# Rotary positions in an attention stage: the halves exchanged by four transfers on SyncE, with weights' high parts on ScalarE from unit three

## The chip, the core and the metric

The kernel runs on one core of a Trainium2 chip. The metric is the time of one execution on the device in microseconds (us); before the change it is 1156.18 us, the median of three runs (1155.56 to 1158.52). The core has five engines with a queue of instructions each: TensorE (PE, with its weight loads as PEld), VectorE (DVE), ScalarE (ACT), GpSimd (POOL) and SyncE (SP). Each works through its own queue in order and waits at an instruction until what this needs is there. Transfers are issued by SP or ACT and carried out by 16 DMA engines.

## The reference, cut to what matters

One inference step of a two-layer decoder with 1024 features: 512 prompt tokens and 8 sample tokens. Layer 0 mixes tokens by sliding-window attention (16 query heads of 64 values, 2 key heads, window 128, a learned sink per head), layer 1 by gated linear attention; each is followed by a gated feed-forward network with a short convolution, and each of the four sublayers by a layer norm. The change touches the attention alone, at the rotary positions, which turn each head's first and second 32 values against each other:

```python
def rope(x, pos):
    ...
    x1, x2 = jnp.split(xf, 2, axis=-1)
    rot = jnp.concatenate([-x2, x1], -1)
    return (xf * cos + rot * sin).astype(x.dtype)
```

So the rotation needs each value's partner, 32 places away in the head.

## The kernel before, in words

Tokens are split into group a (256) and group b (256 + 8). Activations lie with features on the 128 partitions and tokens along the row. Every product of weights is made at higher precision than one pass gives: a weight tile `raw` is split into a high part `wh` and a low part `wl` (`load_unit`, L146 to L162), the activations likewise, and three products of parts are summed in PSUM (`product`, L164 on).

The weights are cut into units of 128 output columns. Unit 0 makes the keys, unit 1 the values, units 2 to 9 eight query chunks of two heads each, units 10 on the output projection, and then come the feed-forward and the second layer. A unit's load is issued by SP into one of two `raw` buffers (RAWS = 2); its parts go to one of six slots (WSLOTS = 6). The high part is made by POOL for units below HIACT = 10 and by ACT from there on; DVE makes the low part. A load has to wait until DVE has finished with the unit two before, and a slot until PE has finished with the unit six before.

In the attention stage (L310 to L532) `attn_k`, `attn_v` and `attn_q` run for each unit and group. Keys and queries go through `rope` (L357 to L369), 18 times in all (keys and eight query chunks, two groups):

- ACT copies the product out of PSUM into `ra` with scale and bias (L362).
- DVE shuffles rows inside blocks of 32 partitions into `rb`, 16 places on (L364). So that partners lie 16 apart within a block of 32, the head's values are laid out in a permuted order, PERM, applied to weights, keys, cache and tables on the host.
- POOL multiplies `ra` by the cosines in place (L365), DVE multiplies `rb` by the sines (L366), POOL adds the two into `rr` (L368).

For a query chunk, ACT makes the high part of `rr` and DVE the low part in `hl` (L413, L414). Four transfers, issued by ACT, put both parts of each head below each other in `qs` (L416 to L419), 64 in all. Then PE makes scores against keys (L446, L447), DVE masks and finds the maximum (L456 to L461), ACT takes exponentials (L463), POOL and DVE normalise (L466, L469), PE transposes (L475), ACT copies (L477), POOL selects the two window halves (L481), and PE multiplies by the values (L494). The tiles `ra`, `rb`, `rr`, `hl` and `qs` have two buffers each, the accumulators `accp` four.

The program's text does not fix the order on each engine. A planner goes through the traced instructions with its own costs and writes every engine's queue in the order in which they came up in its plan; on the chip these orders are fixed. Only the loads at the start keep a given order on SP (`attn_open`, L323 to L346), the loads for units 4 and 5 as the last of them, and a few others are marked to keep program order.

Of the kernel before, what the change touches and what calls it, by code (L numbers as in the profile page):

```python
# [11 lines left out]
F32 = mybir.dt.float32  # L12
# [14 lines left out]
HD = 64  # L27
# [14 lines left out]

WSLOTS = 6
RAWS = 2
HIACT = 10

EXTRA = 1
XEND = 8
# [43 lines left out]
class Net:  # L92
# [53 lines left out]
    def load_unit(self, u, pieces=1, extra=False):  # L146
# [8 lines left out]
        for c in (slice(i * n, (i + 1) * n) for i in range(pieces)):  # L155
            nc.sync.dma_start(out=r[:, c], in_=src[:, c])
            if u >= HIACT:
                nc.scalar.activation(h[:, c], r[:, c], AF.Copy)  # L158
# [198 lines left out]
    def rope(self, g, ps, scale, bias):  # L357
        nc, n = self.nc, g.n
        tab = self.rope_t[:, :, g.c0:g.c0 + n]
        t = lambda name: self.ap.tile([P, NT - 256], F32, name=name, bufs=2)[:, :n]  # L360
        a = t("ra")
        nc.scalar.activation(a, ps, AF.Identity, scale=scale, bias=bias)  # L362
        b = t("rb")
        nc.vector.stream_shuffle(b, a, [(i + 16) % 32 for i in range(32)])  # L364
        nc.gpsimd.tensor_tensor(a, a, tab[:, 0], op=ALU.mult)  # L365
        nc.vector.tensor_tensor(b, b, tab[:, 1], op=ALU.mult)  # L366
        r = t("rr")
        nc.gpsimd.tensor_tensor(r, a, b, op=ALU.add)  # L368
        return r  # L369
# [36 lines left out]
    def attn_q(self, g, u, c):  # L406
        nc = self.nc
# [4 lines left out]
        hl = self.ap.tile([P, 2, 256], F32R, name="hl", bufs=2)  # L412
        nc.scalar.activation(hl[:, 0], r[:, :256], AF.Copy)  # L413
        nc.vector.tensor_tensor(hl[:, 1], r[:, :256], hl[:, 0].bitcast(F32), op=ALU.subtract)  # L414
        qs = self.ap.tile([P, 2, 256], F32R, name="qs", bufs=2)
        for part in range(2):  # L416
            for v in range(2):
                nc.scalar.dma_start(out=qs[64 * part:64 * part + 64, v].bitcast(F32),
                                    in_=hl[64 * v:64 * v + 64, part].bitcast(F32))  # L419
        if g.i:  # L420
            for v in range(2):
                own = slice(64 * v, 64 * v + 64)
# [2 lines left out]
        if g.i and c < 2:  # L425
            if c == 0:
                d = nc.sync.dma_start(out=self.kc[:, :, 0:127], in_=self.I["cache_k"])
            else:
                d = nc.sync.dma_start(out=self.vc, in_=self.I["cache_v"])
# [564 lines left out]

def _perm():
    d = []
    for q in range(2):
        d += list(range(16 * q, 16 * q + 16)) + list(range(32 + 16 * q, 48 + 16 * q))  # L1000
    return np.array(d)


PERM = _perm()
QROWS = np.concatenate([np.concatenate([np.arange(64) + 64 * c, np.arange(64) + 64 * (8 + c)]) for c in range(8)])


def _units(w):

    k, m = w.shape  # L1010
    return np.ascontiguousarray(w.reshape(k // P, P, m // P, P).transpose(2, 1, 0, 3).reshape(m // P, P, k))
# [6 lines left out]
def _consts():  # L1018
# [3 lines left out]
    cos, sin = np.cos(ang), np.sin(ang)  # L1022
    cos = np.concatenate([cos, cos])[PERM]
    sin = np.concatenate([-sin, sin])[PERM]
    cs = np.stack([np.tile(cos, (2, 1)), np.tile(sin, (2, 1))], 1).astype(np.float32)
# [7 lines left out]
def _layout(inp):  # L1033
# [4 lines left out]
    w, b = f["attn_w_qkv"][0], f["attn_b_qkv"][0]  # L1038
    kperm = D + np.concatenate([PERM, 64 + PERM])
    vperm = D + 128 + np.arange(128)  # L1040
    qperm = np.concatenate([np.concatenate([64 * c + PERM, 64 * (8 + c) + PERM]) for c in range(8)])
    order = np.concatenate([kperm, vperm, qperm])
    a["w_qkv"] = _units(w[:, order])
    a["cache_k"] = f["cache_k"][0][:, 1:][..., PERM].transpose(2, 3, 0, 1).reshape(P, NS, 127)

# [58 lines left out]
```

## Time and profile before

| | us |
|---|---|
| median of three runs | 1156.18 |
| the profiled execution | 1155.92 |
| its span, first to last instruction | 1154.2 |
| PE busy in the span | 1106.0 |
| DVE busy | 799.5 |
| ACT busy | 557.3 |
| POOL busy | 348.9 |

The profile shows one execution. "Busy" counts the time in which an engine works; issuing transfers and waiting at them is not counted. A view by stretches gives each engine's busy time between two points of the span. A line such as "L368 POOL ... rr<-ra,rb x18: 721/746/899" is one source line on one engine, what it writes and reads, how often, and the shortest, median and longest duration in ns. "idle before" is the time for which the engine stood idle ahead of those instructions, with what ended it. SPq and ACTq are the queues of SP and ACT, where issues of transfers appear. The chain of waits follows the work that ended last back from one releaser to the one before. The granted clock of TensorE was 0.987 of full over the span.

### The profile page before, as it was taken

The page shows a single profiled execution, that of the slowest core. Times are in us where ns is not written, and L with a number is a line of the kernel's source. Part 1 is how long each engine was busy: PE and PEld are TensorE (multiplying, and loading weights), DVE is VectorE, ACT ScalarE, POOL GpSimd, SP SyncE. Part 2 cuts the span into 40 slices and gives each one's busy share as a digit, 9 for nine tenths or more (in the row PEclk, how much of TensorE's full clock was granted, in tenths as well). Part 3 has the DMA queues.
Part 4 walks back from the last instruction along what each step waited for, and adds up shares of the span by engine and source line. Part 5 has one row for each costly group of instructions (what it writes and reads, how often), then busy time and mean ns, then how long its engine had stood idle before and what let it go on. Part 6 is the DMA issues. An engine that isn't in the chain of part 4 may idle for free.

```text
span 1154.2 us, 22951 instructions
## 1 busy us (share of the span) xinstructions
PE 1106.0 (96%) x8806; PEld 1056.4 (92%) x8806; DVE 799.5 (69%) x1663; ACT 557.3 (48%) x1212; POOL 348.9 (30%) x597
## 2 busy tenths in 40 slices
PE   8988898999999999999899999999999999999995
PEld 7987798999999999998899899889999999999994
DVE  7987769755665456568867777799756665566656
ACT  3455546533554245445545556456533553245433
POOL 4787668200011001156400100378100110010344
PEclk9999999999999999999899999999999999999998
DMA  6634122223323233243034354442323323233212
GB/s 220 177 109 133 25 80 93 92 77 126 110 92 105 97 96 106 73 133 117 29 101 129 126 187 150 142 132 69 110 89 115 108 93 109 93 102 101 74 63 75
DMA packets 53789, 122.82 MB, mean 106 GB/s; under 512 B 6792, under 2 KB 27312, under 8 KB 53680
## 3 DMA queue, kind: packets, MB, share of 16 engines
q1 hardware_dynamic: 46544, 115.41, 30.6%
q10 hardware_dynamic: 7136, 5.95, 2.1%
q8 instruction: 69, 1.13, 0.4%
q14 instruction: 40, 0.33, 0.1%
HBM read 108.67 MB, written 8.47 MB: 101 GB/s over the span
## 4 chain that ended last, share of the span: by engine, by line
PE 72%; DVE 12%; POOL 6%; DMA 4%; issue 3%; ACT 2%; ACTq 0%; SPq 0%; DVEq 0%; POOLq 0%
PE accp L191 15%; PE accp L174 15%; PE accp L173 14%; PE accp L175 14%; PE accp L192 8%; DMA vb<-dv 3%; DVE wl L161 2%; POOL x_b L298 1%; POOL x_a L298 1%; DVE u L296 1%; DVE sgla L845 1%; POOL pr L469 1%; DVE msq L276 1%; PE pv L494 1%; PE sc L767 1%
## 5 line engine op out<-in xcount | busy, mean ns | idle before, releaser
L161 DVE TENSOR_TENSOR wl<-raw,wh 128x1024 fp32r<-128x1024 f32 (+2 forms) x189 | 231.3, 1225 | 106.5 <-ACT wh L158 104.6
L158 ACT ACTIVATE wh<-raw 128x1024 fp32r<-128x1024 f32 (+1 forms) x176 | 182.9, 1039 | 212.4 <-PE accp L174 198.9
L173 PE MATMUL accp<-xh_b,wh 128*128 128x264 f32 x976 | 271.5, 279 | 2.6 <-DVE hprod L600 2.6
L174 PE MATMUL accp<-xl_b,wh 128*128 128x264 f32 x976 | 271.2, 278 | 0.2
L175 PE MATMUL accp<-xh_b,wl 128*128 128x264 f32 x976 | 270.9, 278 | 0.0
L191 PE MATMUL accp<-xs_a,wh 128*128 128x512 f32 x576 | 196.3, 382 | 0.0
L174 PEld LDWEIGHTS accp<-xl_b,wh 128*128 128x128 f32 x976 | 185.2, 190 | 3.3 <-DVE xl_b L301 0.6
L173 PEld LDWEIGHTS accp<-xh_b,wh 128*128 128x128 f32 x976 | 185.1, 190 | 3.3 <-DVE hprod L600 2.9
L175 PEld LDWEIGHTS accp<-xh_b,wl 128*128 128x128 f32 x976 | 184.8, 189 | 0.8 <-issue 0.6
L192 PE MATMUL accp<-xs_a,wl 128*128 128x256 f32 x576 | 145.4, 273 | 0.0
L173 PE MATMUL accp<-hh_b,wh 128*128 128x264 f32 x480 | 133.5, 278 | 2.6 <-ACT hh_b L198 2.6
L174 PE MATMUL accp<-hl_b,wh 128*128 128x264 f32 x480 | 134.0, 279 | 0.0
L175 PE MATMUL accp<-hh_b,wl 128*128 128x264 f32 x480 | 133.2, 277 | 0.0
L191 PEld LDWEIGHTS accp<-xs_a,wh 128*128 128x128 f32 x576 | 109.1, 189 | 11.4
L173 PE MATMUL accp<-xs_a,wh 128*128 128x256 f32 x400 | 113.1, 288 | 4.9 <-DVE x_b L217 1.1
L174 PE MATMUL accp<-xs_a,wh 128*128 128x256 f32 x400 | 112.8, 284 | 3.5 <-DVE xs_a L301 2.9
L175 PE MATMUL accp<-xs_a,wl 128*128 128x256 f32 x400 | 111.7, 282 | 2.9 <-DVE wl L161 2.9
L192 PEld LDWEIGHTS accp<-xs_a,wl 128*128 128x128 f32 x576 | 110.2, 191 | 1.9
L202 POOL COPY hist<-aext 128x2 f32<-128x2 f32 x44 | 8.9, 201 | 284.6 <-DVE aext L578 281.5
L173 PEld LDWEIGHTS accp<-hh_b,wh 128*128 128x128 f32 x480 | 91.2, 190 | 3.1 <-ACT hh_b L198 2.9
L174 PEld LDWEIGHTS accp<-hl_b,wh 128*128 128x128 f32 x480 | 91.1, 190 | 1.5 <-issue 0.3
L175 PEld LDWEIGHTS accp<-hh_b,wl 128*128 128x128 f32 x480 | 91.0, 190 | 0.2
(320 smaller groups left out, 2512.9 us busy)
## 6 DMA issues: line engine op xcount, KB each, us to landing
raw<-in_w_up SPq DMA_DIRECT2D x88, 512.0 KB, 3.4
raw<-in_w_down SPq DMA_DIRECT2D x32, 512.0 KB, 3.4
raw<-in_w_gla SPq DMA_DIRECT2D x24, 512.0 KB, 3.4
raw<-in_w_mix_o SPq DMA_DIRECT2D x16, 512.0 KB, 3.6
raw<-in_w_down SPq DMA_DIRECT2D x16, 384.0 KB, 3.0
qs<-hl ACTq DMA_DIRECT2D x64, 64.0 KB, 2.0
sgla<-in_state_gla SPq DMA_DIRECT2D x16, 256.0 KB, 2.9
vb<-dv SPq DMA_DIRECT2D x16, 256.0 KB, 3.8
```

Of the source, the lines that this page charges most:

```text
L158: nc.scalar.activation(h[:, c], r[:, c], AF.Copy)
L161: nc.vector.tensor_tensor(l[:, c], r[:, c], h[:, c].bitcast(F32), op=ALU.subtract)
L173: nc.tensor.matmul(o, h[:, ks], xh, start=k == 0, stop=False)
L174: nc.tensor.matmul(o, h[:, ks], xl, start=False, stop=False)
L175: nc.tensor.matmul(o, l[:, ks], xh, start=False, stop=k == nt - 1)
L191: both = lambda: nc.tensor.matmul(o, h[:, ks], in_turn(rs[:, k].rearrange("p t q j -> p t (q j)")), start=k == 0, stop=last)
L192: low = lambda: nc.tensor.matmul(o[:, :P], l[:, ks], in_turn(rh[:, k]), start=False, stop=False)
L276: nc.vector.scalar_tensor_tensor(q, q, 0.5, nv, op0=ALU.mult, op1=ALU.mult)
L296: nc.vector.tensor_tensor(u, x[:, m], r, op=ALU.mult)
L298: ts = nc.gpsimd.tensor_scalar(x[:, m], u, sc(m), bi(m), op0=ALU.mult, op1=ALU.add)
L469: nc.gpsimd.tensor_scalar(pr[:, b, 0:P], pr[:, b, 0:P], den[:, b:b + 1], 1.0, op0=ALU.mult, op1=ALU.mult)
L494: mm = nc.tensor.matmul(pv[64 * v:64 * v + 64, b * P:(b + 1) * P], self.vtok[:, kb, 64 * v:64 * v + 64], parts[v][w][:, b], start=i == 0, ...
```

## The change

The shuffle goes. Four transfers of 32 partitions each, issued by SP, write into `rb` the rows of `ra` with neighbouring blocks of 32 exchanged, and the head's values lie in their plain order again (PERM is the identity; the host applies it as before). The 64 transfers into `qs` are issued by SP instead of ACT. HIACT is 2 instead of 10, so that ACT rather than POOL makes the high parts of units 2 to 9, that is from the third unit on; POOL keeps those of units 0 and 1.

```diff
-HIACT = 10
+HIACT = 2
...
         a = t("ra")
         nc.scalar.activation(a, ps, AF.Identity, scale=scale, bias=bias)
         b = t("rb")
-        nc.vector.stream_shuffle(b, a, [(i + 16) % 32 for i in range(32)])
+
+        for i in range(4):
+            nc.sync.dma_start(out=b[32 * i:32 * i + 32], in_=a[32 * (i ^ 1):32 * (i ^ 1) + 32])
         nc.gpsimd.tensor_tensor(a, a, tab[:, 0], op=ALU.mult)
...
         for part in range(2):
             for v in range(2):
-                nc.scalar.dma_start(out=qs[64 * part:64 * part + 64, v].bitcast(F32),
-                                    in_=hl[64 * v:64 * v + 64, part].bitcast(F32))
+                nc.sync.dma_start(out=qs[64 * part:64 * part + 64, v].bitcast(F32),
+                                  in_=hl[64 * v:64 * v + 64, part].bitcast(F32))
...
-def _perm():
-    d = []
-    for q in range(2):
-        d += list(range(16 * q, 16 * q + 16)) + list(range(32 + 16 * q, 48 + 16 * q))
-    return np.array(d)
-
-
-PERM = _perm()
+PERM = np.arange(HD)
```

## Prediction

> **What bounds the kernel now.** I read the page first, then busy time by stretches, then the waits and the chain of waits in the attention stretch, then the tiles that the change touches, and last the timeline around the first and the last rotation.
>
> ```profile
> span 1154.2 us, 22951 instructions
> ...
> PE 1106.0 (96%) x8806; PEld 1056.4 (92%) x8806; DVE 799.5 (69%) x1663; ACT 557.3 (48%) x1212; POOL 348.9 (30%) x597
> ```
>
> TensorE is busy for 96% of the span; the other engines have room only as an average. The rotation (`rope`) lies wholly in the first stage, so the stretches come next. Their columns are start and end, length, busy time of PE, weight load, DVE, ACT and POOL, the granted clock, the DMA engines' share, and GB/s.
>
> ```profile
> core 0: us, PE busy (x) PEld busy (x) DVE busy (x) ACT busy (x) POOL busy (x), PEclk, DMA share, GB/s
> 8.00:28.00 20.00, 16.63 (x117) 14.92 (x117) 18.29 (x37) 8.31 (x21) 10.52 (x14) 0.91 0.66 213
> 28.00:124.00 96.00, 86.93 (x777) 80.37 (x777) 80.97 (x233) 51.64 (x190) 75.38 (x131) 0.98 0.47 134
> 124.00:150.00 26.00, 22.46 (x202) 20.24 (x202) 15.81 (x46) 10.96 (x43) 15.76 (x33) 0.93 0.04 11
> 150.00:1154.00 1004.00, 974.17 (x7692) 935.92 (x7690) 682.23 (x1344) 483.60 (x954) 244.72 (x413) 0.99 0.32 103
> ```
>
> From 28 to 124 us, where the attention heads are worked, PE is idle for 96 - 86.93 = 9.1 us; in the three stretches up to 150 us it is idle for 3.4 + 9.1 + 3.5 = 16.0 us. This is the ceiling on any gain, since the change takes no work from PE and touches nothing after 150 us. In the same 96 us DVE is busy for 81 and POOL for 75: three engines stand at 80 to 90% and feed one another in short steps. What ends the idle time there (total us, times, longest):
>
> ```profile
> ACT hl L413 <- POOL rr L368: 9.3, 4, 3.9
> ...
> PE pv L494 <- POOL pu L481: 6.1, 5, 2.5
> ...
> ACT ra L362 <- POOL rr L368: 4.5, 3, 2.5
> ...
> ACT hl L413 <- DMA qs<-hl: 4.1, 2, 3.4
> ```
>
> No single engine is the bound; ACT waits for POOL's sum and for its own transfers, PE for POOL's selects. The chain of waits from 28 to 120 us, and the one from 20 to 80 us, by share of the stretch:
>
> ```profile
> by line: POOL pr L469 10.2%; issue 7.5%; POOL rr L368 5.7%; POOL pl L481 5.4%; ACTq L418 5.2%; POOL pu L481 5.1%; DVE rb L366 4.8%; DVE wl L161 4.5%; DMA qs<-hl 4.5%; DVE sc L456 3.8%; ACT pr L463 3.5%; DMA raw<-in_w_qkv 3.3%; PE accp L174
> ```
>
> ```profile
> by line: POOL pr L469 9.2%; DVE wl L161 8.2%; issue 6.2%; DVE rb L366 5.8%; DVE xl_b L199 5.1%; DMA raw<-in_w_qkv 5.0%; PE accp L174 4.7%; DVE sc L456 4.6%; DVE rb L364 4.4%; PE accp L175 4.1%; PE accp L173 4.1%; POOL rr L368 3.8%; DVE hl L
> ```
>
> "ACTq L418" is ACT standing at the issue of the qs transfers: 5.2% of 92 us, 4.8 us. "DVE rb L364" is the shuffle: 4.4% of 60 us, 2.6 us.
>
> **The change, part by part.** *The shuffle leaves DVE.*
>
> ```profile
> L364 DVE STREAM_SHUFFLE rb<-ra x18: 430/444/457, 12.8 to 99.3; 128x256 f32<-128x256 f32 x9, 128x264 f32<-128x264 f32 x9
> L366 DVE TENSOR_TENSOR rb<-rb,rope_t x18: 400/496/956, 13.3 to 99.8; 128x256 f32<-128x256 f32 x9, 128x264 f32<-128x264 f32 x9
> L368 POOL TENSOR_TENSOR rr<-ra,rb x18: 721/746/899, 14.9 to 109.9; 128x256 f32<-128x256 f32 x9, 128x264 f32<-128x264 f32 x9
> ```
>
> 18 x 0.444 = 8.0 us of DVE time go. Of these 2.6 us stand on the chain (above); the other 5.4 were covered by other engines already, and I count them at nothing.
>
> *Four transfers take its place.* No row shows an exchange of 32 rows. The nearest transfer is the one of 64 rows from on-chip tile to on-chip tile:
>
> ```profile
> L418 ACTq DMA_DIRECT2D qs<-hl x64: 468/528/1373, 27.1 to 122.9; - x64
> ...
> DMA to landing us min/median/max: 1.9/2.0/6.3
> ```
>
> For issue on SP the nearest row is the weight load:
>
> ```profile
> L156 SPq DMA_DIRECT2D raw<-in_w_qkv x13: 327/328/739, 3.7 to 42.5; - x13
> ```
>
> So one exchange costs three further issues of 0.33 to 0.53 us behind the first, 1.0 to 1.6 us, and then a landing of 2.0 us, less the 0.44 of the shuffle: 2.6 to 3.2 us more for each rotation, from ACT's copy to the start of DVE's product. It also holds POOL's product `a*cos`, which overwrites the source and so has to wait until all four transfers have read it. I take 2.6, from the SP row, because SP issues them. Is it covered? First and last rotation of a query chunk, ACT's copy and POOL's sum:
>
> ```profile
> 12.30 0.47 ACT L362 ACTIVATE ra<-accp,par 128x256 f32<-128x256 f32 x1 [2.83 <-PE accp L175]
> ...
> 20.25 0.47 ACT L362 ACTIVATE ra<-accp,bq 128x256 f32<-128x256 f32 x1 [1.30 <-PE accp L175]
> ```
>
> ```profile
> 25.93 0.73 POOL L368 TENSOR_TENSOR rr<-ra,rb 128x256 f32<-128x256 f32 x1 [0.76 <-DVE rb L366]
> ```
>
> ```profile
> 98.78 0.48 ACT L362 ACTIVATE ra<-accp,bq 128x264 f32<-128x264 f32 x1
> ```
>
> ```profile
> 109.87 0.74 POOL L368 TENSOR_TENSOR rr<-ra,rb 128x264 f32<-128x264 f32 x1
> ```
>
> The query chunk copied at 20.25 has its sum at 25.93, 5.7 us on; the one copied at 98.78 has it at 109.87, 11.1 us on, though the three steps between (0.44, 0.50 and 0.75 us) need 1.7. So the late rotations stand in line for POOL and for the buffers downstream, and another 2.6 us vanishes there. In the early ones there are some 4 us of standing in line, which covers 2.6 if the exchange starts at once; cover gone, each costs up to 2.6.
>
> It does not start at once at the beginning. SP's own loads stand ahead of the first rotation, whose copy is done at 12.30 + 0.47 = 12.8 us:
>
> ```profile
> 15.22 0.45 SPq L344 DMA_DIRECT2D own<-in_own  x1
> ...
> 20.95 0.33 SPq L156 DMA_DIRECT2D raw<-in_w_qkv  x1
> ```
>
> The last of the fixed loads is issued by 15.7 us, and the loads for units four and five, which wait for free raw buffers, go by 21.3. The first exchange starts at one or the other, 2.9 to 8.5 us late. Keys are first used here:
>
> ```profile
> 33.04 0.28 PE L446 MATMUL sc<-khi,qs 128*128 128x256 f32 x1
> ```
>
> At 33.0 there are 11.7 us after even the later start, so the keys themselves cost nothing; but the first query's copy shares two `ra` buffers with them and may move back with them, and PE fills such a hole with the next products only while `ra` and four accumulators allow. Bounds 0 and 8.5 us; I take 2.5, one exchange's delay on the first query, nearer to the lower end because the four accumulators let PE run on meanwhile.
>
> *SP issues the qs transfers.* ACT loses 64 issues of 0.53 us, 34 us, and its waits ahead of them for DVE's low part. All 4.8 us that they hold on the chain go. What is late next is POOL (its `pr`, `rr`, `pl` and `pu` hold 26% of that chain) and then PE. SP takes on 64 + 72 = 136 issues, 45 us at 0.33 and 72 at 0.53, in the 110 us from 13 to 123: it fits, but SP becomes a queue in which things stand behind one another. Behind a waiting exchange stand weight loads; they have room, since the first load of the output projection goes out 41 us before its first product:
>
> ```profile
> 48.90 0.33 SPq L156 DMA_DIRECT2D raw<-in_w_mix_o  x1
> ```
>
> ```profile
> 90.33 0.27 PE L173 MATMUL accp<-hs_a,wh 128*128 128x256 f32 x1
> ```
>
> Behind a waiting weight load stand exchanges; that is the first rival. The DMA engines, at 0.47 in that stretch, take 18 x 128 KB more, which I count at nothing.
>
> *High parts of eight units (three to ten) move from POOL to ACT.* Rows of both:
>
> ```profile
> L160 POOL TENSOR_SCALAR wh<-raw x13: 446/1056/1223, 9.1 to 55.8; 128x1024 fp32r<-128x1024 f32 x7, 128x256 fp32r<-128x256 f32 x4, 128x512 fp32r<-128x512 f32 x2
> L161 DVE TENSOR_TENSOR wl<-raw,wh x13: 411/1212/1765, 10.8 to 57.6; 128x1024 fp32r<-128x1024 f32 x7, 128x256 fp32r<-128x256 f32 x4, 128x512 fp32r<-128x512 f32 x2
> ```
>
> ```profile
> L158 ACT ACTIVATE wh<-raw x13: 1039/1058/1074, 67.8 to 177.6; 128x1024 fp32r<-128x1024 f32 x13
> ```
>
> 8 x 1.06 = 8.5 us leave POOL and come to ACT, at the same price each. ACT has it to give: 11.7 us idle of 20 up to 28 us and 44 of 96 after, before the 34 us of issues go. Cost 0; if ACT stands in its queue for a late load, DVE's low part is late, which at worst is another 1 to 2 us in the startup (range). The gain on POOL is bounded by 8.5; I take 0, since no wait for `wh` stands among the long waits above.
>
> POOL's products run from 0.74 to 2.29 us, and POOL stood idle ahead of them for 9.4 us until a shuffle had read the source:
>
> ```profile
> L365 POOL TENSOR_TENSOR ra<-ra,rope_t x18: 736/888/2293, 13.3 to 101.0; 128x256 f32<-128x256 f32 x9, 128x264 f32<-128x264 f32 x9
> ...
> L365 POOL TENSOR_TENSOR ra<-ra,rope_t 128x256 f32<-128x256 f32 (+1 forms) x18 | 18.4, 1022 | 11.3 <-DVE rb L364 9.4 <-DVE small L464 1.8
> ```
>
> and DVE's low part from 0.41 to 1.77 (the row above, median 1.21), so the two slow each other. [...]
>
> **Sum.** -2.6 (shuffle) - 4.8 (ACT's issues) + 2.5 (late start) = -4.9 us on the profiled execution, which took 1155.92 us (span 1154.2 and 1.7 around it): 1151.0. The median of the three runs, 1156.18, is 0.26 above it; the forecast is 1151 us. A measurement of this kernel can tell about 0.3%, 3.5 us, from no change.
>
> **The rivals.** *SP's queue becomes the wait (slower).* SP issues in order. A weight load that waits for its raw buffer holds every exchange queued behind it, and a load on its way delays their landing:
>
> ```profile
> raw<-in_w_up SPq DMA_DIRECT2D x88, 512.0 KB, 3.4
> ```
>
> A landing of 3.4 instead of 2.0 makes an exchange 4.0 us longer than the shuffle rather than 2.6. POOL then stands in order at `a*cos`, with the selects behind it that PE waits for, as it did once already:
>
> ```profile
> 80.54 0.70 PE L494 MATMUL pv<-pu,vtok 128*64 128x128 f32 x4 [2.54 <-POOL pu L481]
> ```
>
> The rotations before 80 us, some twelve, have the least slack. If half of them pass 2.6 us on to PE, this is +15.6, and with -7.4 + 2.5 + 0 the sum is +10.7 at most; I set this case at +8, 1164 us. It decides as soon as the 18 rotations pass on more than 7.4 / 18 = 0.4 us each. For it: each rotation now crosses two transfers in one in-order queue, and POOL already waited 9.4 us on the shuffle. Against it: the late rotations' 11 us, and weight loads that run 41 us ahead. [...]
>
> *PE takes the place (no change).* The chain's 7.4 us fall to PE, which is 91% busy from 28 to 124: what is saved ahead of a matmul is waited for behind it, or the late start eats all of it (5 us of the 0 to 8.5). Then 1153 to 1159, at 1156.
>
> **How the numbers follow.** Faster as forecast 0.43, SP's queue 0.37, PE in its place 0.20. I put the forecast a little ahead since three crowded engines lose work (8 us, 8.5 us, 34 us of issues) and only latency is added, most of it in line with a queue. The range runs from the sum with the port's 4.4 us and no late start, 1151 - 4.4 - 2.5 = 1144, to the slower case with a few us more of startup, 1170. The likeliest case's own range is 1144 to 1153.
>
> **What would show it.** Right: no ACTq L418 in the chain of waits, PE idle from 28 to 124 near 5 us, ACT never behind qs, POOL waiting for rb no longer than 9 us in all. Wrong: long waits of POOL L365 or DVE L366 for a transfer into `rb`, exchanges landing above 3 us, SP's queue waiting on raw buffers with exchanges behind, the first scores after 38 us, or PE idle above 16 us in the first 150. The forecast also fails if anything after 150 us moves by more than a microsecond or two, since nothing there is touched.

## The result and the profile after

The changed kernel takes 1169.37 us, the median of four runs (1165.66 to 1172.86); the kernel before takes 1155.87 beside it (four runs, 1154.15 to 1158.52). The ratio is 1.0105 with a 95% interval of 1.0085 to 1.0125: slower by 13.5 us, where 5 us less had been forecast. The profiled execution took 1170.28 us, with a span of 1168.6. Its line numbers behind L364, the shuffle of before, are two higher: L366 is now the exchange on SP, L367 and L368 are the products with cosine and sine, L370 is the sum, L415 the high part, L420 the transfers into `qs`, L448 and L449 the scores.

The page of the changed kernel:

```profile
span 1168.6 us, 23093 instructions
...
PE 1111.7 (95%) x8806; PEld 1057.5 (90%) x8806; DVE 789.7 (68%) x1627; ACT 568.4 (49%) x1221; POOL 337.3 (29%) x588
```

DVE and POOL have lost the work that they were to lose (9.8 and 11.6 us; 8.0 and 8.5 had been counted), ACT works 11.1 us more. PE counts 5.7 us more of busy time for the same 8806 matmuls. The same kernel by stretches, with the columns of the view of before:

```profile
core 0: us, PE busy (x) PEld busy (x) DVE busy (x) ACT busy (x) POOL busy (x), PEclk, DMA share, GB/s
8.00:28.00 20.00, 17.34 (x138) 15.98 (x139) 14.88 (x27) 11.93 (x24) 6.78 (x8) 1.00 0.76 254
28.00:124.00 96.00, 80.55 (x670) 72.42 (x669) 63.72 (x173) 49.52 (x161) 53.83 (x102) 0.96 0.47 133
124.00:164.00 40.00, 33.10 (x289) 27.63 (x287) 25.76 (x80) 18.94 (x76) 27.47 (x56) 1.00 0.17 44
164.00:1168.00 1004.00, 974.32 (x7688) 936.06 (x7688) 682.81 (x1344) 484.56 (x954) 246.50 (x413) 0.99 0.32 103
```

The last 1004 us hold 974.32 us of PE work; those of before held 974.17. Nothing behind the attention stage moved. The stage itself ends 14.4 us later, at 1168.6 - 1004.2 = 164.4 instead of 150.0. From 28 to 124 us PE is idle for 15.5 us (9.1 before), and runs 670 matmuls where it ran 777. What ended the idle times in the first 165 us (total us, times, longest):

```profile
POOL ra L367 <- DMA rb<-ra: 33.8, 7, 12.6
...
DVE rb L368 <- DMA rb<-ra: 12.2, 6, 5.2
...
PEld accp L173 <- ACT ra L362: 7.8, 8, 2.6
...
PE accp L173 <- ACT ra L362: 6.1, 6, 2.4
```

POOL and DVE wait for the exchange. The last two lines carry the cost further: the products of the next unit (`accp`, L173) wait for ACT's copy into `ra` (L362), which frees an accumulator. Before, no such line stood among the long waits. The startup is not the reason: the scores begin at 32.93 us, against 33.04 before. The timeline of PE around the first score:

```profile
32.59 0.28 PE L175 MATMUL accp<-xh_b,wl 128*128 128x264 f32 x1
32.70 0.28 PE L173 MATMUL accp<-xh_b,wh 128*128 128x264 f32 x1
32.81 0.28 PE L174 MATMUL accp<-xl_b,wh 128*128 128x264 f32 x1
32.93 0.29 PE L448 MATMUL sc<-khi,qs 128*128 128x256 f32 x1
```

These four rows also say how PE's busy time is to be read. In a dense row a matmul starts every 0.11 us, though each lasts 0.28; one that stands alone counts its whole length (the one at 7.99 us its 0.35). Matmuls that come apart therefore add to the busy time without any more work.

Why does ACT's copy come late? One turn of the rotation's loop, first SP's queue, then ACT, DVE and POOL:

```profile
101.97 7.25 SPq L420 DMA_DIRECT2D qs<-hl  x8
109.32 4.98 SPq L366 DMA_DIRECT2D rb<-ra  x8
```

```profile
101.72 0.47 ACT L362 ACTIVATE ra<-accp,bq 128x264 f32<-128x264 f32 x1
...
106.03 0.46 ACT L362 ACTIVATE ra<-accp,bq 128x264 f32<-128x264 f32 x1
...
116.36 0.46 ACT L362 ACTIVATE ra<-accp,bq 128x264 f32<-128x264 f32 x1
...
120.29 0.47 ACT L362 ACTIVATE ra<-accp,bq 128x264 f32<-128x264 f32 x1
```

```profile
113.22 0.43 DVE L368 TENSOR_TENSOR rb<-rb,rope_t 128x264 f32<-128x264 f32 x1 [1.58 <-DMA rb<-ra]
```

```profile
115.22 0.77 POOL L370 TENSOR_TENSOR rr<-ra,rb 128x264 f32<-128x264 f32 x1
```

The copy at 101.72 is done at 102.2. Its exchange starts at 109.32, since eight `qs` transfers stand ahead of it in SP's queue; its product follows at 113.22, its sum ends at 115.99, and the next copy into that buffer starts at 116.36: 14.6 us for one turn of two buffers, 7.3 us per rotation. Over all 18, a rotation takes 12.1 us on average from the start of the copy to the end of the sum (7.1 before), and the copies come 7.03 us apart (5.09 before). The last one:

```profile
130.35 0.47 ACT L362 ACTIVATE ra<-accp,bq 128x264 f32<-128x264 f32 x1
```

That is 31.6 us later than the 98.78 of before, for a stage that ends 14.4 us later.

### The profile page after: what moved, and what is told of

It is laid out like the page before. It is cut to its first block, busy times and chain, and to the rows that moved or that the text cites. A ratio compares the mean times of both kernels' runs of the same rounds, so it can differ in the third digit from the quotient of the medians.

```text
span 1168.6 us, 23093 instructions
## 1 busy us (share of the span) xinstructions
PE 1111.7 (95%) x8806; PEld 1057.5 (90%) x8806; DVE 789.7 (68%) x1627; ACT 568.4 (49%) x1221; POOL 337.3 (29%) x588
## 4 chain that ended last, share of the span: by engine, by line
PE 67%; DVE 9%; issue 3%; DMA 3%; POOL 3%; ACT 2%; SPq 0%; ACTq 0%; DVEq 0%; POOLq 0%
PE accp L191 15%; PE accp L174 14%; PE accp L175 14%; PE accp L173 14%; PE accp L192 7%; DMA vb<-dv 3%; DVE wl L161 2%; POOL x_b L298 1%; POOL x_a L298 1%; DVE sgla L847 1%; DVE u L296 1%; DVE msq L276 1%; PE sc L769 0%; PE pv L780 0%; DVE de L862 0%
## 5 line engine op out<-in xcount | busy, mean ns | idle before, releaser
L158 ACT ACTIVATE wh<-raw 128x1024 fp32r<-128x1024 f32 (+2 forms) x185 | 191.9, 1038 | 218.9 <-PE accp L174 201.4
L173 PE MATMUL accp<-xh_b,wh 128*128 128x264 f32 x976 | 273.8, 281 | 8.1 <-ACT ra L362 5.2
L173 PEld LDWEIGHTS accp<-xh_b,wh 128*128 128x128 f32 x976 | 186.4, 191 | 10.3 <-ACT ra L362 6.0
L173 PE MATMUL accp<-hh_b,wh 128*128 128x264 f32 x480 | 133.3, 278 | 1.0 <-ACT hh_b L198 1.0
L191 PEld LDWEIGHTS accp<-xs_a,wh 128*128 128x128 f32 x576 | 109.1, 189 | 11.4
L173 PE MATMUL accp<-xs_a,wh 128*128 128x256 f32 x400 | 112.5, 287 | 5.3 <-DVE x_b L217 1.1
L173 PEld LDWEIGHTS accp<-hh_b,wh 128*128 128x128 f32 x480 | 90.9, 189 | 1.6 <-ACT hh_b L198 1.5
```

The source lines that it names most:

```text
L173: nc.tensor.matmul(o, h[:, ks], xh, start=k == 0, stop=False)
L191: both = lambda: nc.tensor.matmul(o, h[:, ks], in_turn(rs[:, k].rearrange("p t q j -> p t (q j)")), start=k == 0, stop=last)
```

## The experiments

The theory: the exchange lengthens the loop from ACT's copy to POOL's sum, and since `ra` and `rb` have two buffers each, a longer loop means fewer rotations per time; PE starves. Against it stood: the weight loads that share SP's queue (the rival of the prediction), `qs` now sharing it as well, the other two edits as such, and the mere traffic of 72 more transfers.

**The change without its exchange, and the exchange without the rest.** All diffs stand against the changed kernel, and where the shuffle is back, PERM of before is back with it. First the shuffle in place of the exchange:

```diff
-        for i in range(4):
-            nc.sync.dma_start(out=b[32 * i:32 * i + 32], in_=a[32 * (i ^ 1):32 * (i ^ 1) + 32])
+        nc.vector.stream_shuffle(b, a, [(i + 16) % 32 for i in range(32)])
```

> The changed kernel with DVE's shuffle and the permuted layout put back; SP still issues the qs transfers and HIACT stays 2. Theory 'exchange' (the four transfers alone make the loss, through SP's queue or through the two buffers): 1151 to 1158 us, attention stage over by about 148 us. Rival 'other edits' (the move of the qs transfers to SP, or ACT's high parts, makes a good part of it): 1162 us or more.

Measured: 1151.29 us (1150.06 to 1153.05, four runs), ratio 0.9948 [0.9929, 0.9967]. Without the exchange the change gains 5.2 us of 1156.5; the exchange costs 1169.37 - 1151.29 = 18.1. Its stretch from 28 to 124 us and its last copy:

```profile
28.00:124.00 96.00, 88.01 (x794) 80.72 (x795) 78.12 (x240) 57.05 (x205) 67.28 (x129) 1.00 0.46 131
```

```profile
94.52 0.48 ACT L362 ACTIVATE ra<-accp,bq 128x264 f32<-128x264 f32 x1 [0.35 <-POOL rr L368]
```

794 matmuls in the stretch instead of 670, and the last copy 36 us earlier. Then the exchange alone, with the rest as before:

```diff
-HIACT = 2
+HIACT = 10
...
-                nc.sync.dma_start(out=qs[64 * part:64 * part + 64, v].bitcast(F32),
+                nc.scalar.dma_start(out=qs[64 * part:64 * part + 64, v].bitcast(F32),
```

> The kernel before with the four transfers of the exchange on SP and nothing else: ACT issues the qs transfers, HIACT is 10. Theory 'queue' (on SP the exchange stands behind qs transfers that wait for hl, and 0.58 us for each issue): without qs on SP the exchange starts at once, 1154 to 1161. Theory 'ring' (two ra and rb buffers over a loop that is longer by issue and landing): 1162 to 1170. Rival 'other edits': 1156.

Measured: 1168.78 us (1164.51 to 1171.97, four runs), ratio 1.0101 [1.0068, 1.0133]. The exchange alone is as slow as the whole change. So the other two edits, worth 5.2 us under the shuffle, are worth nothing measurable under the exchange.

**The queue.** `qs` goes back to ACT, and in another kernel the four transfers of an exchange alternate between SP and ACT:

```diff
-                nc.sync.dma_start(out=qs[64 * part:64 * part + 64, v].bitcast(F32),
+                nc.scalar.dma_start(out=qs[64 * part:64 * part + 64, v].bitcast(F32),
```

> The changed kernel with the qs transfers issued by ACT again; exchange on SP, HIACT 2. 'queue': 1154 to 1161, exchanges issued within 1 us of ACT's copy. 'ring': 1162 to 1170, PE still waiting for ACT's copy. 'other edits' with qs as the culprit: 1156.

```diff
-            nc.sync.dma_start(out=b[32 * i:32 * i + 32], in_=a[32 * (i ^ 1):32 * (i ^ 1) + 32])
+            (nc.sync, nc.scalar)[i % 2].dma_start(out=b[32 * i:32 * i + 32], in_=a[32 * (i ^ 1):32 * (i ^ 1) + 32])
```

> The changed kernel with two of the four transfers of each exchange issued by SP and two by ACT. 'queue' as issue time (4 x 0.59 us in a row on SP): 1.2 us less for each rotation and less on SP, 1160 to 1165. If ACT's place in its own queue costs as much again: 1167 to 1173.

Measured: 1166.87 us (1164.96 to 1173.77), ratio 1.0097 [1.0063, 1.0132], and 1169.42 (1166.12 to 1170.95), ratio 1.0099 [1.007, 1.0129], four runs each. Both lie inside the interval of the change. With `qs` on ACT a rotation shortens from 12.1 to 9.4 us, and the time hardly moves: the queue is part of the loop's length and not the cause by itself. What SP waited for in the changed kernel, in its first 165 us, shows which transfers held the queue:

```profile
SPq L420 <- ACT ra L362: 15.4, 11, 3.3
SPq L420 <- ACT hh_b L198: 7.0, 1, 7.0
SPq L156 <- DVE wl L161: 4.7, 3, 2.5
```

The first two rows are 22 us at transfers into `qs` (L420) until ACT had got on, with exchanges behind them. Over all rows of this view it is 31 us at L420 and 10 at the weight loads (L156), 4.7 of these for a raw buffer that DVE still read.

**The buffers.** A third buffer for `ra` and `rb`; three small tiles move into room that the layer norm leaves free, so that this fits:

```diff
-        t = lambda name: self.ap.tile([P, NT - 256], F32, name=name, bufs=2)[:, :n]
+        t = lambda name: self.ap.tile([P, NT - 256], F32, name=name, bufs=3 if name != "rr" else 2)[:, :n]
...
-        vt = self.ap.tile([P, NT - 256], F32, name="ra", bufs=2)[:, :n]
+        vt = self.ap.tile([P, NT - 256], F32, name="ra", bufs=3)[:, :n]
...
-            self.vs = self.ap.tile([NS, P], F32, name="vs")
+            self.vs = self.ln.tile([P, NT - 256], F32, name="nv", bufs=1)[:NS, :P]
...
-        pr = self.ap.tile([P, P], F32, name="prs")
+        pr = self.ln.tile([P, NT - 256], F32, name="msq", bufs=1)[:, :P]
...
-        pt = self.ap.tile([P, P], F32, name="pts")
+        pt = self.ln.tile([P, NT - 256], F32, name="r", bufs=1)[:, :P]
```

> The changed kernel with three buffers instead of two for ra and rb (three small tiles of the sample tokens lie in layer-norm scratch to make room). 'ring': the products no longer wait for ACT's copy, 1154 to 1162. 'queue': SP still issues 136 transfers in order behind waits, the pace stays near 7 us for each rotation, 1165 or more.

The same three buffers, with `qs` on ACT:

```diff
-                nc.sync.dma_start(out=qs[64 * part:64 * part + 64, v].bitcast(F32),
+                nc.scalar.dma_start(out=qs[64 * part:64 * part + 64, v].bitcast(F32),
```

> The changed kernel with both remedies: three buffers for ra and rb, and ACT issues the qs transfers. If 'queue' and 'ring' are two separate parts (2.5 and 4.7 us by their own runs): 1160 to 1163. If a transfer's latency inside the chain costs time even with room in both: not below 1160. If the two remedies together free the loop: 1154 to 1158.

And the three buffers where there is no exchange:

```diff
-        for i in range(4):
-            nc.sync.dma_start(out=b[32 * i:32 * i + 32], in_=a[32 * (i ^ 1):32 * (i ^ 1) + 32])
+        nc.vector.stream_shuffle(b, a, [(i + 16) % 32 for i in range(32)])
```

> The kernel of e1 with three buffers for ra and rb. If two buffers bind only where the exchange makes the loop long: as e1, 1150 to 1153. If they bind with the shuffle too: 1146 to 1149, and the gain in e4 is no evidence on the exchange.

Measured, four runs each: 1164.70 us (1162.04 to 1166.72), ratio 1.0066 [1.0043, 1.009]; 1166.67 (1164.11 to 1169.19), 1.0077 [1.005, 1.0103]; without the exchange 1150.32 (1149.45 to 1151.78), 0.9947 [0.993, 0.9964], the same as with two buffers. Under the exchange the third buffer brings the pace of the copies from 7.03 to 5.95 us and the last copy from 130.4 to 111.8, so the ring of two did set the pace. Of the time it returns 4.7 us of 18.1, with intervals that just overlap. The ring is then at most part of the cost, and the two remedies together are no better than one. With `qs` on ACT and two buffers the late copies do not even wait for the ring. In that kernel this sum frees a buffer of `ra`, and these rows of ACT lead to the copy that fills it:

```profile
99.72 0.72 POOL L370 TENSOR_TENSOR rr<-ra,rb 128x256 f32<-128x256 f32 x1
```

```profile
101.17 1.15 ACTq L420 DMA_DIRECT2D qs<-hl  x2
102.37 0.37 ACT L465 ACTIVATE pr<-sc,small 128x129 f32<-128x129 f32 x1 [2.35 <-DVE small L463]
...
104.98 0.50 ACT L362 ACTIVATE ra<-accp,bq 128x264 f32<-128x264 f32 x1
```

The buffer is free at 100.4 and filled from 104.98 on: the copy stands in ACT's own fixed order, behind issues into `qs` and exponentials. The last eight copies of that kernel come 1.0 to 5.0 us after a buffer came free, and it still loses 15.6 us to the version without exchange.

**The number of transfers.** One transfer of 128 rows, or two of 64, in place of the four. The first copies each row to its own place and the second exchanges heads instead of halves, so both leave the rotation out and stand for the time alone:

```diff
-        for i in range(4):
-            nc.sync.dma_start(out=b[32 * i:32 * i + 32], in_=a[32 * (i ^ 1):32 * (i ^ 1) + 32])
+        for i in range(1):
+            nc.sync.dma_start(out=b[128 * i:128 * i + 128], in_=a[128 * i:128 * i + 128])
```

> The changed kernel with one transfer of 128 rows instead of four of 32, so that rows are copied and not exchanged (each value is its own partner in the rotation). Same bytes, same landing, one issue instead of four. Theory 'issue' (the four issues in a row and SP's time make the loss): 1152 to 1157. Theory 'landing' (some 2 us in the loop, however issued): 1163 to 1168.

```diff
-        for i in range(4):
-            nc.sync.dma_start(out=b[32 * i:32 * i + 32], in_=a[32 * (i ^ 1):32 * (i ^ 1) + 32])
+        for i in range(2):
+            nc.sync.dma_start(out=b[64 * i:64 * i + 64], in_=a[64 * (i ^ 1):64 * (i ^ 1) + 64])
```

> The changed kernel with two transfers of 64 rows, which exchange the two heads of a chunk and not the halves of each. 'issue': between one transfer and four, 1157 to 1163. 'landing': 1165 to 1169, as with four.

One transfer, with the three buffers of above:

```diff
-        for i in range(4):
-            nc.sync.dma_start(out=b[32 * i:32 * i + 32], in_=a[32 * (i ^ 1):32 * (i ^ 1) + 32])
+        for i in range(1):
+            nc.sync.dma_start(out=b[128 * i:128 * i + 128], in_=a[128 * i:128 * i + 128])
```

> The kernel of e13 (rows copied, not exchanged) with three buffers for ra and rb. If landing still binds through the two buffers: 3 us or more under e13. If issue was all: as e13.

Measured: one transfer 1167.16 us (1165.87 to 1167.74, four runs), ratio 1.0084 [1.0052, 1.0117]; two 1172.50 (1169.56 to 1173.81, four runs), 1.0125 [1.0095, 1.0156]; one with three buffers 1164.37 (1162.64 to 1167.15, seven runs), 1.0067 [1.0047, 1.0087]. The last copy of each, in that order:

```profile
112.25 0.87 ACT L362 ACTIVATE ra<-accp,bq 128x264 f32<-128x264 f32 x2
```

```profile
122.76 0.46 ACT L362 ACTIVATE ra<-accp,bq 128x264 f32<-128x264 f32 x1
```

```profile
91.89 0.48 ACT L362 ACTIVATE ra<-accp,bq 128x264 f32<-128x264 f32 x1
```

With the shuffle, one, two and four transfers the last copy of the profiled execution starts at 94.5, 112.6 (the row above holds the last two together), 122.8 and 130.4 us: the more transfers, the slower the pace. The time does not follow in the same way. A single transfer already costs 15.9 of the 18.1 us, and between two and four there is no difference that could be told. So most of the price is that there is a transfer in the loop at all. How much of the 15.9 a single transfer would cost that nobody reads was not tried. With three buffers the last copy comes earlier than the shuffle's (91.9), and 13.1 of the 15.9 us still stay.

**Early or late rotations.** The exchange by transfers (here eight of 16 rows, so that both forms can share one order of the values) for query chunks four to seven only, then for the keys and chunks zero to three only; the others keep the shuffle. The diff is that of the late ones (`c`, the number of the chunk, is passed to `rope`); the other kernel has `c < 4` in it:

```diff
-        for i in range(4):
-            nc.sync.dma_start(out=b[32 * i:32 * i + 32], in_=a[32 * (i ^ 1):32 * (i ^ 1) + 32])
+        if c >= 4:
+            for i in range(8):
+                nc.sync.dma_start(out=b[16 * i:16 * i + 16], in_=a[16 * (i ^ 1):16 * (i ^ 1) + 16])
+        else:
+            nc.vector.stream_shuffle(b, a, [(i + 16) % 32 for i in range(32)])
```

> The kernel of e1 with transfers instead of the shuffle for the query chunks 4 to 7 alone (8 rotations; in the permuted layout an exchange takes 8 transfers of 16 rows, 64 in all). The prediction's claim that the late rotations stand in line anyway: 1151 to 1155. Rival, every rotation pays because the transfer lengthens the loop that hands the next one its buffers: 1157 to 1163.

> The kernel of e1 with transfers for the keys and the query chunks 0 to 3 alone (10 rotations, 80 transfers). The prediction's claim: the loss lies here, 1160 to 1168. Rival: no more for each rotation than in the late ones, 1157 to 1163.

Measured, four runs each: 1176.08 us (1173.16 to 1178.23), ratio 1.0167 [1.0141, 1.0192], and 1188.17 (1186.79 to 1189.23), 1.0276 [1.0257, 1.0295]. Over the 1151.29 without exchange, eight late rotations cost 24.8 us, 3.1 each, and ten early ones 36.9, 3.7 each. The late ones are not covered, with eight transfers each; with four they were not run apart. Eight of 16 rows also cost more than four of 32: the two kernels together lose 61.7 us with 144 transfers, the change 18.1 with 72.

**Transfers that nobody reads.** The version without exchange, with 72 transfers of `rr` into a tile that nothing reads (the three small tiles move as above, to make room for it):

```diff
+        rd = self.ap.tile([P, NT - 256], F32, name="rd", bufs=1)[:, :n]
+        for i in range(4):
+            nc.sync.dma_start(out=rd[32 * i:32 * i + 32], in_=r[32 * (i ^ 1):32 * (i ^ 1) + 32])
```

> The kernel of e1 (shuffle, qs on SP, HIACT 2) with 72 further transfers of the exchange's shape on SP, out of the rotated rows into a tile that nobody reads. Theory 'latency in the chain': the same number of transfers without a reader costs little, 1151 to 1155. Rival 'load on SP and the DMA engines': 1160 or more.

Measured: 1159.73 us (1155.34 to 1161.13, ten runs), ratio 1.0009 [0.9994, 1.0025], 8.4 us over the version without them (7 by the two ratios). The traffic, its issues and the new order of the queues are not free, even with no one reading the result. They are less than half of the 18.1, and mostly by another way, as the table below shows. They are not quite without a waiter: POOL's next sum stood 2.5 us in all until they had read `rr`.

**The other edits alone.** With the shuffle, only `qs` on SP:

```diff
-        for i in range(4):
-            nc.sync.dma_start(out=b[32 * i:32 * i + 32], in_=a[32 * (i ^ 1):32 * (i ^ 1) + 32])
+        nc.vector.stream_shuffle(b, a, [(i + 16) % 32 for i in range(32)])
...
-HIACT = 2
+HIACT = 10
```

> The kernel before with the qs transfers issued by SP and nothing else. If ACT's freed queue is what gives e1 its 5 us: 1151 to 1153. If ACT's high parts give it: 1155 to 1157.

With the shuffle, only HIACT = 2:

```diff
-        for i in range(4):
-            nc.sync.dma_start(out=b[32 * i:32 * i + 32], in_=a[32 * (i ^ 1):32 * (i ^ 1) + 32])
+        nc.vector.stream_shuffle(b, a, [(i + 16) % 32 for i in range(32)])
...
-                nc.sync.dma_start(out=qs[64 * part:64 * part + 64, v].bitcast(F32),
+                nc.scalar.dma_start(out=qs[64 * part:64 * part + 64, v].bitcast(F32),
```

> The kernel before with HIACT 2 and nothing else. With qs on SP alone 1.8 us under before and both together 5.2 us under: if the two add up, 1152 to 1155; if ACT, still issuing qs, has no room for the high parts, 1156 or more.

Measured, ten runs each: 1154.83 us (1153.16 to 1157.07), ratio 0.9984 [0.9972, 0.9997], and 1157.11 (1153.38 to 1159.13, and one run of 5532 that the ratio leaves out), 0.9996 [0.9983, 1.0009]. Alone they gain 1.8 us and nothing, together 5.2. One reading is that ACT has room for the high parts only once it no longer issues the transfers; no run separates that.

**Where the time goes, in one table.** From each profiled execution: the mean rotation (start of the copy to end of the sum), the same divided by the buffers, the pace (first to last copy over 17), how many copies start within 0.6 us of a buffer of `ra` coming free (of 17 that can wait for one, 16 with three buffers; the copies of the values hold a buffer too), and for the stage its end (span less 1004.2), PE's idle time from 8 us on, the time lost to the granted clock (busy time times one minus the clock, in stretches of 2 us) and the rest, all times in us.

| kernel | rotation | per buffer | pace | at once | stage end | PE idle | clock | rest |
|---|---|---|---|---|---|---|---|---|
| before | 7.1 | 3.6 | 5.09 | 8 | 150.0 | 16.0 | 4.6 | 121.4 |
| no exchange | 6.5 | 3.3 | 4.89 | 6 | 147.1 | 12.9 | 1.7 | 124.5 |
| one transfer | 9.5 | 4.7 | 5.98 | 12 | 159.9 | 23.2 | 4.6 | 124.1 |
| two transfers | 10.8 | 5.4 | 6.60 | 9 | 166.5 | 22.6 | 10.9 | 125.0 |
| four (the change) | 12.1 | 6.1 | 7.03 | 13 | 164.4 | 25.0 | 3.4 | 128.1 |
| four, `qs` on ACT | 9.4 | 4.7 | 6.61 | 5 | 160.7 | 22.0 | 6.0 | 124.7 |
| no exchange, three buffers | 7.5 | 2.5 | 4.49 | 0 | 143.3 | 10.6 | 4.0 | 120.7 |
| one, three buffers | 10.9 | 3.6 | 4.79 | 7 | 156.7 | 17.1 | 6.2 | 125.4 |
| four, three buffers | 15.8 | 5.3 | 5.95 | 7 | 160.3 | 20.4 | 8.9 | 123.0 |
| four, three buffers, `qs` on ACT | 11.4 | 3.8 | 5.76 | 1 | 158.9 | 23.4 | 7.0 | 120.5 |
| unread transfers | 7.3 | 3.7 | 5.46 | 7 | 154.8 | 13.2 | 6.1 | 127.6 |

With two buffers the pace is half the rotation and 1.0 to 1.9 us more, in each of these rows. In the changed kernel 13 of 17 copies start as soon as a buffer is free, in the kernel before 8. With `qs` on ACT there are no more of them than with the shuffle, and PE is idle nearly as long. Under the exchange with two buffers PE's idle time rises by 9 to 12 us over the version without it; with three, by 6 to 13 over the version without it that has three as well. The unread transfers add none to the idle time: they cost by the clock and by the rest, which holds PE's work itself and grows where its matmuls come apart.

**What is shown and what is open.** Shown: the exchange is the whole of the loss, one transfer in the loop is most of it, and the late rotations pay too (3.1 us each with eight transfers). In the changed kernel the two buffers set the pace of the rotations. They are not the cause by themselves: with `qs` on ACT the copies wait in ACT's order instead, and the loss is nearly the same. Open: by which waits the added latency reaches PE where the copies no longer wait for buffers, and why the time stays high once the pace is back. In the kernel with one transfer and three buffers PE's gaps lie partly among the rotations (5.4 us idle from 60 to 100 us, 2.0 without the exchange), partly behind them (5.3 us from 132 to 148, where the version without the exchange has one gap of 2.6), and the granted clock falls behind them (0.57 from 136 to 140, 0.50 from 148 to 152). The planner orders every queue anew for each kernel, and an order that suits the exchange less well is a candidate; that was not tried.

## Why the prediction was wrong, step by step

- **The step that failed** is that the late rotations "stand in line for POOL and for the buffers downstream, and another 2.6 us vanishes there". The 11 us from copy to sum were read as room. A rotation that stands in line holds a buffer of `ra` and `rb`, and where both are held, its length sets when the next can begin. The prediction named the two buffers for the startup alone. Among its own rows stood ACT's copy waiting 4.5 us for POOL's sum, and late rotations of the kernel before show where:

```profile
78.81 0.48 ACT L362 ACTIVATE ra<-accp,bq 128x264 f32<-128x264 f32 x1 [1.55 <-POOL rr L368]
...
82.05 0.48 ACT L362 ACTIVATE ra<-accp,bq 128x264 f32<-128x264 f32 x1 [2.49 <-POOL rr L368]
```

  There the next copy already waited for a rotation to end, so what makes that rotation longer delays the copy. As a rate, 12.1 us over two buffers is 6.05 us, above the 5.09 at which the copies came before. Late rotations, with eight transfers each, cost 3.1 us apiece where the step had nothing.
- **The price of an exchange** was too low with it. The landing was right: 1.9 us at the median, 2.0 taken. The issue was not: taken from the weight load's row at 0.33, it is 0.59 (0.51 to 2.05), so the three further issues take 1.8 us instead of 1.0. The wait in SP's queue, 7 us in the turn shown above, was not in the sum at all. The tile's view in the changed kernel:

```profile
L366 SPq DMA_DIRECT2D rb<-ra x72: 507/588/2050, 11.3 to 137.4; - x72
...
DMA to landing us min/median/max: 1.8/1.9/6.1
```

- **ACT's issues, -4.8**: under the shuffle the two other edits gain 5.2 together. The total came near, its parts did not: 1.8 for the issues alone, and the high parts, which stood at nothing and gain nothing alone, bring the rest together with them. Under the exchange none of it is left.
- **The shuffle, -2.6**: no run shows a gain from DVE's freed 8 us, and none separates it from the exchange. DVE then waited 12.2 us for transfers.
- **The late start, +2.5**: the first scores came 0.1 us earlier, so the term was about nothing. Of the first exchange's four transfers one was issued at 11.31 us and three from 16.02 on, behind the fixed loads, which is the earlier of the two starts considered; the room ahead of the first scores took all of it.
- **The port's 4.4 us**, the low end of the range, are a term that no run shows: they were the author's estimate of what DVE's low parts would gain with eight POOL instructions less. The runs showed little of it. The row of 0.41 to 1.77 us that the estimate took mixes pieces of three sizes; these are the large ones alone, before and with the high parts alone moved:

```profile
L161 DVE TENSOR_TENSOR wl<-raw,wh 128x1024 fp32r<-128x1024 f32 x7 | 10.4, 1480 | 0.2 <-POOL wh L160 0.2
```

```profile
L161 DVE TENSOR_TENSOR wl<-raw,wh 128x1024 fp32r<-128x1024 f32 x8 | 11.1, 1393 | 1.0 <-ACT wh L158 1.0
```

  A large piece takes 0.09 us less in the mean, 0.6 us for seven of them, and the two middle ones (128x512) take 0.27 us more each (1.22 against 0.95).
  The interval of that kernel's time, 0.9983 to 1.0009, leaves no room for a gain of 4.4 us, 0.4%. The longest of POOL's cosine products did fall, from 2.29 to 1.01 us. That DVE's low parts and POOL's products slow each other shows in the kernel before, though not everywhere: a large piece took 1.23 us with POOL idle (at 19.69 us), and beside busy POOL 1.76 (at 32.79) or 1.21 (at 47.66); a cosine product took 0.74 us with DVE idle (at 80.46) and 2.29 beside DVE (at 68.90).
- **The first rival**, SP's queue, had the sign (+8 priced, +13.5 measured), but its two means show only in part. Weight loads held SP for some 10 us against 31 at `qs`, and at the median the landing did not lengthen (1.9 us, 2.0 for `qs` before). Some exchanges did land late with a load on its way: the two transfers issued at 16.02 and 16.61 us, right behind the weight load of 15.58, landed after 5.8 and 6.1 us, that load itself after 6.1. Those issued from 109.32 to 113.72, with no load on its way, took 1.8 to 1.9. The longer wait was ahead of the issue, in SP's own order behind `qs`, 7 us in the turn shown above.
- **The signs to look for** did their work. POOL waited 33.8 us for `rb` (the bound was 9), PE was idle 25.0 us in the stage (16), and nothing behind the stage moved (974.32 against 974.17). Of the other signs of being wrong, late landings showed in part (1.9 us at the median, 6.1 at most), and the late scores stayed away (32.93).

## What to carry to other kernels

A step inside a loop over n buffers is checked as a rate: the loop's new length over n, against the pace at which the work now comes. Waiting inside that loop is no cover, since it holds the buffer. The check is a warning and not a price: for the single transfer it gives 4.7 us, below the 5.09 of before, and 15.9 us were lost all the same. So ask as well what stands behind the longer step in each engine's fixed order. Even one transfer that lands in 2.1 us at the median, in place of a 0.44 us shuffle, cost 1.4% here, in a stage where PE was busy for nine tenths. The other two edits are worth keeping with the shuffle: 1151.29 us, ratio 0.9948 [0.9929, 0.9967], beats both kernels, and a third buffer adds nothing to it.

## What the runs showed of the hardware

Behind some short gaps of PE the granted clock was lower for a while, and what that cost came on top of the gap. The changed kernel in stretches of 1 us:

```profile
36.00:37.00 1.00, 0.83 (x8) 0.64 (x6) 0.41 (x2) 0.00 (x0) 0.36 (x1) 1.00 0.12 34
37.00:38.00 1.00, 0.00 (x0) 0.00 (x0) 0.97 (x4) 0.00 (x0) 0.92 (x2) 1.00 0.36 91
38.00:39.00 1.00, 0.00 (x0) 0.00 (x0) 1.00 (x3) 0.56 (x2) 1.00 (x2) 1.00 0.77 274
39.00:40.00 1.00, 0.73 (x6) 0.73 (x7) 1.00 (x1) 0.22 (x1) 0.15 (x1) 0.99 0.48 193
40.00:41.00 1.00, 1.00 (x7) 1.00 (x7) 1.00 (x5) 0.00 (x0) 0.00 (x0) 0.50 0.56 126
...
43.00:44.00 1.00, 1.00 (x9) 1.00 (x9) 0.95 (x4) 0.96 (x3) 0.25 (x2) 0.80 0.51 125
44.00:45.00 1.00, 1.00 (x10) 0.86 (x8) 0.97 (x3) 0.95 (x4) 0.00 (x0) 1.00 0.20 48
```

PE stands still for some 2.4 us, and from 40 us on the granted clock is 0.50 for three microseconds and 0.80 in the fourth: 1.7 us lost behind a gap of 2.4. In the kernel with unread transfers a gap of 2.0 us, from 34.0 on, was followed by a clock of 0.50 from 38 to about 48 us, with further gaps in that time:

```profile
34.00:35.00 1.00, 0.01 (x1) 0.00 (x0) 0.98 (x5) 0.14 (x1) 0.83 (x2) 1.00 0.57 127
35.00:36.00 1.00, 0.00 (x0) 0.00 (x0) 0.76 (x2) 1.00 (x6) 0.00 (x0) 1.00 0.15 38
...
38.00:39.00 1.00, 0.60 (x2) 0.20 (x2) 0.96 (x4) 0.36 (x2) 0.68 (x2) 0.50 0.84 143
39.00:40.00 1.00, 0.11 (x2) 0.11 (x4) 0.74 (x3) 1.00 (x7) 0.76 (x2) 0.50 0.90 341
...
47.00:48.00 1.00, 1.00 (x6) 1.00 (x6) 0.00 (x0) 0.00 (x0) 0.00 (x0) 0.50 0.40 93
48.00:49.00 1.00, 1.00 (x9) 0.92 (x8) 0.00 (x0) 0.00 (x0) 0.00 (x0) 0.90 0.35 79
```

So the granted clock was 0.50 behind gaps of 2.4 and 2.0 us. It was not behind every such gap: behind one of 2.5 us in the kernel with two transfers, from 44.5 on, and one of 1.9 in the changed kernel, from 48.3 on, it stayed at 1.00. What decides between them the runs do not show. Over the stage the lower clock cost 1.7 us without the exchange and 15.6 with eight transfers for each early rotation, the other kernels of the table between them. That is part of why the times of like experiments do not line up with the pace of their rotations: the table has 10.9 us for two transfers and 3.4 for four.
